# Feed-forward in a tuned encoder kernel: gate and up of seven chunks as a block product with seven half products

## The chip, the cores and the metric

The kernel runs on one core of a Trainium2 chip. The metric is the time of one execution on the device in microseconds. The kernel before takes 1268.14 us as the median of three runs (1267.69 to 1270.22).

TensorE is PE in the profile (its weight loads are PEld), VectorE is DVE, ScalarE is ACT, GpSimd is POOL and SyncE is SP.

## The reference

Two layers run over one sequence of 256 tokens with a width of 1024. Each layer is a half-step feed-forward, a mixer (a gated recurrence beside a forgetting attention), and a second half-step feed-forward. All is float32. The feed-forward is what matters here:

```
def rms_norm(x, g):
    y = x * rsqrt(mean(x * x, axis=-1) + EPS)
    return y * g

def swiglu_ffn(h, w_up, w_down):           # h 256 x 1024, D_FF = 2816
    gate, up = split(h @ w_up, 2, axis=-1) # w_up 1024 x 5632
    return (silu(gate) * up) @ w_down      # w_down 2816 x 1024

x = x + 0.5 * swiglu_ffn(rms_norm(x, g_ffn1[l]), w_up1[l], w_down1[l])
...                                        # the mixer
x = x + 0.5 * swiglu_ffn(rms_norm(x, g_ffn2[l]), w_up2[l], w_down2[l])
```

## The kernel before

**Products in float32.** TensorE multiplies a shortened format (`float32r`). So every operand is split into a high part and the rest, `hi` and `lo`, and a product is three matmuls: hi x hi, hi x lo, lo x hi (L398 to L400 in `visit`). The activations are split once, as `xT` (the tokens in the columns of the stationary operand, 128 at a time, so there are two token halves). The weights are the moving operand and are split as they come.

**Weight tiles.** `plan` and its callers put the weights of the whole program into one list, `hcs`, in the order of use. An entry is 512 KB: two blocks of 128 rows by 512 columns (a `raw` tile of 128 x 1024 elements). For each entry SP issues a load into one of four `raw` buffers (`emit_dma`, L299), ACT casts it to `whi` (`emit_hi`, L332), DVE subtracts that from `raw` to give `wlo` (`emit_lo`, L341) and with that frees the `raw` buffer for the next load. There are six `whi` and six `wlo` buffers. `can_hi` lets the cast of an entry be written out only after the entry six places before has been used by both token halves.

**Feed-forward.** `plan_ffn` and `ffn` go through six chunks of 512 of the 2816 inner columns (the last has 256). For each chunk, `block` makes the gate and then the up product: for each token half four weight tiles are summed into one PSUM bank. When a bank is full, `ev_g` applies silu with the scale rstd on ACT, and `ev_u` multiplies by the up product on DVE. `h_chain` turns the result (`turn`: a copy on ACT or DVE, a DMA transpose issued by SP, a copy back) and splits it. After the up product of chunk c (c from 1 to 4), `down` adds chunk c - 1 into four banks held through the whole feed-forward (`x` and `y`).

**What sets the order.** The program is written out by a planner, `Sched`, in Python. It keeps an expected time for PE, ACT, DVE and POOL, adds a fixed cost for each instruction it writes (`act_c`, `dve_c`), and works with generators: a `Chain` yields the time from which it is ready and the engine that it needs next. After each 512 columns of a weight tile `visit` calls `hook`, which first lets `split` cast and subtract the next weight tile, at most three ahead, then steps the chains that are ready, background ones (`bg`) only if their engine is not more than 2.5 us ahead, and then lets `split` go further ahead, up to the ring's size, if the engine has little to do. What comes out is one fixed list of instructions for each engine, and each engine runs its list strictly in that order.

**Buffers besides.** Twelve `slot` buffers of 8 KB per partition hold the larger tiles (`s0` to `s11` in the rows); four PSUM banks `z` serve gate, up and transposes. `rows_chain` loads the small constants through POOL into a slot, waits 70 us of planned time, and transposes them on PE.

## Time and profile before

| | |
|---|---|
| median of three runs | 1268.14 us |
| the profiled execution | 1271.76 us |
| its span | 1270.0 us |
| PE, PEld busy | 1255.3 us (99%), 1033.6 us (81%) |
| DVE, ACT busy | 824.9 us (65%), 826.8 us (65%) |
| DMA | 253.5 MB, 200 GB/s on average |

The span goes from the first to the last instruction of the program on the core; the execution's own time is 1.76 us longer. A busy share is an average over stages that differ much: feed-forward takes four stretches, each between two mixers or at the ends. Matmuls are pipelined, and the end of each is modelled, so rows of PE overlap and the start of one after the other is what a matmul costs. A wait is put down to what came last.

### The profile page before, as it was taken

What the parts mean: (1) busy time and instruction counts of PE and PEld (TensorE: products, weight loads), DVE (VectorE), ACT (ScalarE), POOL (GpSimd) and SP (SyncE); (2) the same over time, 40 slices, a digit from 0 to 9 for tenths busy, and PEclk for the clock granted to TensorE, in tenths of its full rate; (3) what the DMA queues carried; (4) which work ended last, traced back from release to release, by engine and by line L of the source; (5) the groups of instructions that cost most, each with busy time, mean ns of one, the idle gap of its engine ahead of it and who ended that gap; (6) DMA issues with size and microseconds to landing.
All of it is one profiled execution on the core that took longest, in us unless ns stands there. A gap on an engine that the chain in (4) does not pass through costs nothing.

```text
span 1270.0 us, 16219 instructions
## 1 busy us (share of the span) xinstructions
PE 1255.3 (99%) x5889; PEld 1033.6 (81%) x5889; DVE 824.9 (65%) x1158; ACT 826.8 (65%) x1086; POOL 68.6 (5%) x88
## 2 busy tenths in 40 slices
PE   9999999999999999999999999999999999999998
PEld 7887887788877888888878888878887778888887
DVE  6655556798777666555475555578987767655553
ACT  6657556886799456555566555569768984665553
POOL 4000000001400000000000000000032000000000
PEclk9999999999999999999999999999999999999999
DMA  7977769576567568667768677596676665687773
GB/s 252 247 212 217 223 173 257 142 222 208 166 174 188 178 190 212 205 213 206 193 195 238 199 207 207 157 276 163 203 218 156 184 189 174 200 223 215 215 189 102
DMA packets 212304, 253.50 MB, mean 200 GB/s; under 512 B 92488, under 2 KB 104960, under 8 KB 212224
## 3 DMA queue, kind: packets, MB, share of 16 engines
q1 hardware_dynamic: 210288, 249.21, 67.8%
q0 software_dynamic: 1920, 3.26, 1.2%
q8 instruction: 46, 0.75, 0.3%
q14 instruction: 34, 0.28, 0.1%
q10 hardware_dynamic: 16, 0.00, 0.0%
HBM read 229.88 MB, written 2.10 MB: 183 GB/s over the span
## 4 chain that ended last, share of the span: by engine, by line
PE 72%; DVE 5%; DMA 2%; issue 1%; ACT 1%; SPq 0%; DVEq 0%; ACTq 0%
PE x L398 11%; PE x L400 11%; PE x L399 11%; PE z L398 9%; PE z L400 9%; PE z L399 9%; PE y L398 3%; PE y L400 3%; PE y L399 3%; DVE wlo L341 2%; PE z L1010 1%; PE z L479 1%; PE y L1082 1%; DMA tmp<-in_b_gate_dram 1%; PE z L820 1%
## 5 line engine op out<-in xcount | busy, mean ns | idle before, releaser
L341 DVE TENSOR_TENSOR wlo<-raw,whi 128x1024 fp32r<-128x1024 f32 x423 | 510.2, 1221 | 220.6 <-ACT whi L332 213.3
L332 ACT CAST whi<-raw 128x1024 fp32r<-128x1024 f32 x423 | 439.5, 1048 | 208.4 <-PE z L400 122.0
L398 PE MATMUL x<-whi,s 128*128 128x512 f32 x800 | 323.3, 404 | 5.5 <-ACT s L500 2.4
L399 PE MATMUL x<-wlo,s 128*128 128x512 f32 x800 | 312.9, 391 | 0.8 <-DVE wlo L341 0.7
L400 PE MATMUL x<-whi,s 128*128 128x512 f32 x800 | 313.3, 392 | 0.1
L398 PE MATMUL z<-whi,s 128*128 128x512 f32 (+1 forms) x752 | 279.6, 372 | 1.0 <-ACT s L500 1.0
L399 PE MATMUL z<-wlo,s 128*128 128x512 f32 (+1 forms) x752 | 279.8, 372 | 0.1
L400 PE MATMUL z<-whi,s 128*128 128x512 f32 (+1 forms) x752 | 279.6, 372 | 0.0
L398 PEld LDWEIGHTS x<-whi,s 128*128 128x128 f32 x800 | 150.4, 188 | 40.9 <-ACT s L500 4.7
L400 PEld LDWEIGHTS x<-whi,s 128*128 128x128 f32 x800 | 150.4, 188 | 34.9 <-DVE s L502 2.5
L399 PEld LDWEIGHTS x<-wlo,s 128*128 128x128 f32 x800 | 150.6, 188 | 30.9 <-DVE wlo L341 2.0
L399 PEld LDWEIGHTS z<-wlo,s 128*128 128x128 f32 x752 | 141.8, 189 | 26.0 <-DVE wlo L341 1.8
L398 PEld LDWEIGHTS z<-whi,s 128*128 128x128 f32 x752 | 141.8, 189 | 25.6 <-ACT s L500 1.4
L400 PEld LDWEIGHTS z<-whi,s 128*128 128x128 f32 x752 | 141.8, 189 | 25.0 <-DVE s L502 0.8
L319 ACT COPY tmp<-nat 128x1024 uint16<-128x1024 uint16 (+1 forms) x88 | 96.3, 1114 | 75.9 <-DMA nat<-tmp 67.9
L398 PE MATMUL y<-whi,s 128*128 128x512 f32 x208 | 82.4, 396 | 0.0
L400 PE MATMUL y<-whi,s 128*128 128x512 f32 x208 | 81.1, 390 | 0.0
L399 PE MATMUL y<-wlo,s 128*128 128x512 f32 x208 | 81.1, 390 | 0.0
L640 DVE SCALAR_TENSOR_TENSOR nat<-z,rstd,nat 128x512 f32<-128x512 f32 (+1 forms) x48 | 33.9, 705 | 56.3 <-PE z L400 56.3
L502 DVE TENSOR_TENSOR s<-tmp,s 128x512 fp32r<-128x512 f32 (+1 forms) x71 | 46.6, 656 | 34.8 <-ACT s L500 34.4
L500 ACT CAST s<-tmp 128x512 fp32r<-128x512 f32 (+1 forms) x71 | 42.1, 594 | 28.1 <-DVE tmp L529 26.5
L635 ACT ACTIVATE nat<-z,rstd 128x512 f32<-128x512 f32 (+1 forms) x46 | 29.9, 651 | 45.1 <-PE z L400 45.0
(164 smaller groups left out, 903.1 us busy)
## 6 DMA issues: line engine op xcount, KB each, us to landing
raw<-in_w_up_dram SPq DMA_DIRECT2D x175, 512.0 KB, 4.7
...
```

Of the source, the lines that this page charges most:

```text
L319: nc.scalar.copy(out_, in_)
L332: nc.scalar.copy(hi, raws[i])
L341: nc.vector.tensor_tensor(out=lo, in0=raws.pop(i), in1=f32(hi), op=ALU.subtract)
L398: nc.tensor.matmul(acc, lhsT=lhs(0, k0 + kk)[:, ts], rhs=hi[:, kk, :], start=st, stop=False)
L399: nc.tensor.matmul(acc, lhsT=lhs(0, k0 + kk)[:, ts], rhs=lo[:, kk, :], start=False, stop=False)
L400: nc.tensor.matmul(acc, lhsT=lhs(1, k0 + kk)[:, ts], rhs=hi[:, kk, :], start=False, stop=sp)
L479: nc.tensor.transpose(dst_ps[:, j * P:(j + 1) * P], src[:, j * P:(j + 1) * P], ident)
L500: nc.scalar.copy(hi, t)
L502: nc.vector.tensor_tensor(out=lo, in0=t, in1=f32(hi), op=ALU.subtract)
L635: nc.scalar.activation(s[tok][0], acc, AF.Silu, scale=rs(tok))
L640: nc.vector.scalar_tensor_tensor(out=h, in0=acc, scalar=rs(tok), in1=h, op0=ALU.mult, op1=ALU.mult)
L820: nc.tensor.matmul(ps[:, g, :], lhsT=wax[0][:, g, n, :], rhs=xr[0][:, n, :], start=True, stop=True)
```

## The change

Gate and up of a chunk are seen as one product of 2 x 2 blocks: the activations are split by token half and by the upper and lower half of the 1024 inputs, the weights by that same half and by gate or up. The four result blocks (gate and up of each token half) are then made of seven products of blocks instead of eight, after the scheme of Strassen and Winograd. A product of blocks is here two weight tiles by one token half.

- `SEVEN` names the chunks: chunk 3 in the first feed-forward, chunks 2 and 4 in the other three.
- The weight blocks are `11` (gate, upper half), `12` (up, upper), `22` (up, lower), `21` (gate, lower). They are loaded straight into slots, in twos (`u` 0 and 1) of 512 KB, each two together with one of the `raw` loads ahead of them (`plan_seven`, `emit_dma`).
- `Seven.sums` makes on DVE t3 = 22 - 12, t1 = 12 - 11 (over `12`), t2 = t3 + 11 (over `11`, after `11` has been split) and t4 = 21 - t2 (over `21`, after that has been split). It starts as a background chain 6 us of planned time after the last load was written.
- The seven weights `11`, t1, t2, `21`, t3, `22`, t4 are split into `whi` and `wlo` like any tile: 14 entries instead of 8, each used by one product.
- `sums_chain` makes the four sums of activations once in each feed-forward, and splits them.
- In `seven(c)` the products come into `z` banks; ACT copies the first, DVE makes seven additions, and then silu, the multiplication and `h_chain` follow as before.
- `rows_chain` waits 25 us of planned time instead of 70.

```diff
@@ -48,6 +48,8 @@
+SEVEN = ((3,), (2, 4), (2, 4), (2, 4))
@@ -237,9 +239,77 @@
     def plan(w, r0, c0, nk, ncol):
-        hcs.append((w[r0:r0 + nk * P, c0:c0 + ncol].rearrange("(k p) n -> p k n", p=P), nk, ncol))
+        loads.append((w[r0:r0 + nk * P, c0:c0 + ncol].rearrange("(k p) n -> p k n", p=P), len(hcs)))
+        hcs.append((nk, ncol))
+        uses.append(NT)
+
+    ORDER = ("11", "t1", "t2", "21", "t3", "22", "t4")
...
+        def load(self, name, u, src):
...
+            nc.sync.dma_start(out=self.part(name, u), in_=src)
+            if name != "12":
+                raws[self.index(name, u)] = self.part(name, u), 0.0
+            if (name, u) == ("21", 1):
+                self.chain = S.add(self.sums(), S.now + 6.0, "d", True)
+
+        def sums(self):
+            def op(name, u, dst, a, b, f):
+                o = self.part(dst, u)
+                nc.vector.tensor_tensor(out=o, in0=self.part(a, u), in1=self.part(b, u), op=f)
+                raws[self.index(name, u)] = o, S.use("d", dve_c(1024))
+
+            for u in range(2):
+                op("t3", u, "t3", "22", "12", ALU.subtract)
+                yield S.now, "d"
+                op("t1", u, "12", "12", "11", ALU.subtract)
+                yield S.now, "d"
+            for name, dst, a, b, f in (("t2", "11", "t3", "11", ALU.add), ("t4", "21", "21", "11", ALU.subtract)):
+                for u in range(2):
+                    while nxt["lo"] <= self.index(dst, u):
+                        yield S.now + 0.5, "d"
+                    op(name, u, dst, a, b, f)
+                    yield S.now, "d"
...
+    def plan_seven(w, f0):
...
+        for name, r0, c0 in (("11", 0, f0), ("12", 0, FF + f0), ("22", 512, FF + f0), ("21", 512, f0)):
+            for u in range(2):
+                r = r0 + 256 * u
+                loads.insert(len(loads) - 3 + n // 2, (w[r:r + 256, c0:c0 + 512].rearrange("(k p) n -> p k n", p=P),
+                                                       (st, name, u)))
+                n += 1
+        for _ in range(14):
+            hcs.append((2, 512))
+            uses.append(1)
@@ -297,16 +370,18 @@
     def emit_dma(cuts=1):
...
+        while loads and isinstance(loads[0][1], tuple):
+            src, (st, name, u) = loads.pop(0)
+            st.load(name, u, src)
@@ -322,31 +397,33 @@
     def can_hi():
         i = nxt["hi"]
-        return i < NHC and i in raws and (i < RING or used[i - RING] == NT)
+        return i < NHC and i in raws and (i < RING or used[i - RING] == uses[i - RING])
...
-        emit_dma()
+        if uses[i] == NT:
+            emit_dma()
@@ -624,6 +706,115 @@
+        def sums_chain():
...
+            for q in range(2):
...
+                nc.vector.tensor_tensor(out=a[0][:, ks], in0=f32(xh[:, ks]), in1=f32(xl[:, ks]), op=ALU.add)
...
+            for i, u, v, f in ((0, A(1, 0), A(1, 1), ALU.add), (1, B(0), A(0, 0), ALU.subtract),
+                               (2, A(0, 0), A(1, 0), ALU.subtract), (3, A(0, 1), B(1), ALU.subtract)):
...
+                yield from split_seg(b[0][:, ii], sums[0][0][:, ii], sums[1][0][:, ii], 1024)
...
+        def seven(c):
...
+            def prod(name, lhs_, fin):
+                b, r = zbank()
+                for u in range(2):
+                    visit(st.index(name, u), b, lhs_, 2 * u, None, u == 0, u == 1, (lambda: fin(b, r)) if u else None)
...
+            def after_1(b, r):
+                nc.scalar.copy(s1, b)
...
+            def after_6(b, r):
+                plus(u2, b, s1)
+                r.free = True
+                plus(u4, b5[0], u2)
+
+            def after_2(b, r):
+                end = plus(s1, b, s1)
+                r.free = True
+                gate(0, s1, end)
+
+            def after_7(b, r):
+                plus(u2, b, u2)
+                r.free = True
+                plus(c22, b5[0], u2)
+                b5[1].free = True
+
+            def after_3(b, r):
+                end = plus(u4, b, u4)
+                r.free = True
+                up(0, u4, end)
+
+            def after_4(b, r):
+                end = plus(u2, b, u2)
+                r.free = True
+                up(1, c22, gate(1, u2, end))
+
+            prod("11", xh(0, 0), after_1)
+            prod("t1", xs(0), lambda b, r: b5.extend((b, r)))
+            prod("t2", xs(1), after_6)
+            prod("21", xh(0, 1), after_2)
+            prod("t3", xs(2), after_7)
+            prod("22", xs(3), after_3)
+            prod("t4", xh(1, 1), after_4)
...
@@ -1212,7 +1407,7 @@
-        yield S.now + 70.0, "p"
+        yield S.now + 25.0, "p"
```

**The order, place 1: DVE in the second feed-forward, from chunk 1's up block to the first weights of chunk 2.** Before, where `raw_810` to `raw_820` are tiles of the down product and `raw_825` is the first of chunk 2's gate:

```order
L341 TENSOR_TENSOR wlo_826_4286<-raw_810_4189,whi_822_4263 128x1024
L640 SCALAR_TENSOR_TENSOR nat_812_4216<-z_823_4265,rstd_107,nat_812_4216 128x512
L316 COPY tmp_830_4309<-nat_812_4216 128x1024
L341 TENSOR_TENSOR wlo_831_4318<-raw_816_4234,whi_829_4307 128x1024
L341 TENSOR_TENSOR wlo_835_4332<-raw_820_4252,whi_833_4322 128x1024
L640 SCALAR_TENSOR_TENSOR nat_821_4261<-z_828_4300,rstd_107,nat_821_4261 128x512
L341 TENSOR_TENSOR wlo_838_4345<-raw_825_4271,whi_834_4330 128x1024
L341 TENSOR_TENSOR wlo_841_4353<-raw_827_4288,whi_837_4343 128x1024
L341 TENSOR_TENSOR wlo_848_4395<-raw_832_4320,whi_845_4377 128x1024
```

After the change, in the same place. `raw_836`, `raw_842` and `raw_845` belong to the down product; `s4` holds `11` and then t2, `s8` holds `12` and then t1, `s0` holds `22`, `s3` holds t3, and `s1` will hold `21` and t4. Tiles are numbered in the text by the place of their `wlo` in DVE's list: that of `raw_836` is tile 169, `raw_842` and `raw_845` are 170 and 171, and the seven are 172 to 185 (the first two are the `wlo` from `s4` below). Chunk 1 has the tiles 160 to 167.

```order
L416 TENSOR_TENSOR wlo_852_4350<-raw_836_4253,whi_849_4337 128x1024
L279 TENSOR_TENSOR s3_832_4243<-s0_830_4241,s8_829_4240 128x1024
L279 TENSOR_TENSOR s8_829_4240<-s8_829_4240,s4_828_4239 128x1024
L279 TENSOR_TENSOR s3_832_4243<-s0_830_4241,s8_829_4240 128x1024
L831 SCALAR_TENSOR_TENSOR nat_838_4281<-z_848_4333,rstd_107,nat_838_4281 128x512
L279 TENSOR_TENSOR s8_829_4240<-s8_829_4240,s4_828_4239 128x1024
L416 TENSOR_TENSOR wlo_856_4383<-raw_842_4302,whi_855_4381 128x1024
L416 TENSOR_TENSOR wlo_861_4406<-raw_845_4315,whi_858_4393 128x1024
L831 SCALAR_TENSOR_TENSOR nat_847_4331<-z_854_4373,rstd_107,nat_847_4331 128x512
L416 TENSOR_TENSOR wlo_865_4423<-s4_828_4239,whi_860_4404 128x1024
L279 TENSOR_TENSOR s4_828_4239<-s3_832_4243,s4_828_4239 128x1024
L416 TENSOR_TENSOR wlo_868_4442<-s4_828_4239,whi_863_4417 128x1024
```

Five sums stand among the subtractions here, four of them ahead of tile 170, and every later `wlo` of DVE stands behind them.

**Place 2: DVE at the end of the same seven.** Here `s7` holds the four partial results, `z_889` is the product with t2, `z_885` with t1, `z_893` with `21`, `z_898` with t3, `z_902` with `22`; the last `wlo` of a seven is that of `s1` before `raw_851`, the first down tile (186).

```order
L757 TENSOR_TENSOR s7_879_4499<-z_889_4545,s7_879_4499 128x512
L757 TENSOR_TENSOR s7_879_4499<-z_885_4525,s7_879_4499 128x512
L416 TENSOR_TENSOR wlo_894_4570<-s3_832_4243,whi_888_4543 128x1024
L416 TENSOR_TENSOR wlo_896_4580<-s0_830_4241,whi_890_4552 128x1024
L757 TENSOR_TENSOR s7_879_4499<-z_893_4566,s7_879_4499 128x512
L416 TENSOR_TENSOR wlo_899_4592<-s0_830_4241,whi_892_4564 128x1024
L416 TENSOR_TENSOR wlo_900_4600<-s1_831_4242,whi_895_4575 128x1024
L757 TENSOR_TENSOR s7_879_4499<-z_898_4588,s7_879_4499 128x512
L757 TENSOR_TENSOR s7_879_4499<-z_885_4525,s7_879_4499 128x512
L416 TENSOR_TENSOR wlo_903_4613<-s1_831_4242,whi_901_4607 128x1024
L416 TENSOR_TENSOR wlo_905_4623<-raw_851_4345,whi_904_4618 128x1024
L757 TENSOR_TENSOR s7_879_4499<-z_902_4609,s7_879_4499 128x512
```

Additions that wait for a product of PE now stand between the `wlo` of the next products; before, each bank of four weight tiles was read by one instruction of ACT or DVE.

**Place 3: SP in the same stretch.** Before:

```order
L308 DMA raw_806_4180<-in_w_down2_dram 128x2x512
L308 DMA raw_810_4189<-in_w_down2_dram 128x2x512
L515 DMA_TRANSPOSE nat_790_4099<-tmp_811_4194 128x8x128
L308 DMA raw_816_4234<-in_w_down2_dram 128x2x512
L308 DMA raw_820_4252<-in_w_down2_dram 128x2x512
L308 DMA raw_825_4271<-in_w_up2_dram 128x2x512
L308 DMA raw_827_4288<-in_w_up2_dram 128x2x512
L515 DMA_TRANSPOSE nat_812_4216<-tmp_830_4309 128x8x128
L308 DMA raw_832_4320<-in_w_up2_dram 128x2x512
```

After; `x2` is two loads of 512 KB:

```order
L380 DMA raw_827_4237<-in_w_down2_dram 128x2x512
L270 DMA s4_828_4239<-in_w_up2_dram 128x2x512 x2
L380 DMA raw_836_4253<-in_w_down2_dram 128x2x512
L270 DMA s8_829_4240<-in_w_up2_dram 128x2x512 x2
L597 DMA_TRANSPOSE nat_807_4144<-tmp_837_4260 128x8x128
L380 DMA raw_842_4302<-in_w_down2_dram 128x2x512
L270 DMA s0_830_4241<-in_w_up2_dram 128x2x512 x2
L380 DMA raw_845_4315<-in_w_down2_dram 128x2x512
L270 DMA s1_831_4242<-in_w_up2_dram 128x2x512 x2
L380 DMA raw_851_4345<-in_w_down2_dram 128x2x512
```

Two loads of a seven follow each of four `raw` loads. In these rows the first transpose of h has six loads ahead of it, in those of before two.

## Rows read from the trace of the kernel before

**Rows 1.** The page: busy time by engine (part 1), TensorE's granted clock (part 2).

```profile
PE 1255.3 (99%) x5889; PEld 1033.6 (81%) x5889; DVE 824.9 (65%) x1158; ACT 826.8 (65%) x1086; POOL 68.6 (5%) x88
PEclk9999999999999999999999999999999999999999
```

**Rows 2.** The page, part 4: shares of the chain that ended last.

```profile
PE 72%; DVE 5%; DMA 2%; issue 1%; ACT 1%; SPq 0%; DVEq 0%; ACTq 0%
```

**Rows 3.** Busy time of each engine in two feed-forward windows; columns in the heading.

```profile
core 0: us, PE busy (x) PEld busy (x) DVE busy (x) ACT busy (x) POOL busy (x), PEclk, DMA share, GB/s
508.00:540.00 32.00, 32.00 (x142) 26.48 (x142) 17.74 (x17) 17.51 (x19) 0.00 (x0) 1.00 0.69 204
540.00:572.00 32.00, 32.00 (x143) 26.50 (x142) 17.74 (x17) 17.73 (x19) 0.00 (x0) 1.00 0.68 213
```

**Rows 4.** Timeline of PE in feed-forward: start us, us, engine, line, operation, tiles.

```profile
79.73 0.39 PE L398 MATMUL z<-whi,s 128*128 128x512 f32 x1
...
82.00 0.39 PE L399 MATMUL z<-wlo,s 128*128 128x512 f32 x1
```

**Rows 5.** Waits of the weight loads on VectorE: us in total, times, longest us.

```profile
PEld x L399 <- DVE wlo L341: 2.0, 3, 1.1
...
PEld z L399 <- DVE wlo L341: 1.8, 5, 0.5
```

**Rows 6.** Groups by line and shape: busy us, mean ns of one, idle before.

```profile
L341 DVE TENSOR_TENSOR wlo<-raw,whi 128x1024 fp32r<-128x1024 f32 x423 | 510.2, 1221 | 220.6 <-ACT whi L332 213.3
L332 ACT CAST whi<-raw 128x1024 fp32r<-128x1024 f32 x423 | 439.5, 1048 | 208.4 <-PE z L400 122.0 <-PE x L400 43.3 <-DMA raw<-in_w_in_dram 12.2
L640 DVE SCALAR_TENSOR_TENSOR nat<-z,rstd,nat 128x512 f32<-128x512 f32 x40 | 30.0, 750 | 45.9 <-PE z L400 45.9
L635 ACT ACTIVATE nat<-z,rstd 128x512 f32<-128x512 f32 x38 | 26.2, 689 | 43.4 <-PE z L400 43.4
L316 DVE COPY tmp<-nat 128x1024 uint16<-128x1024 uint16 x24 | 16.7, 698 | 5.7 <-DMA nat<-tmp 5.0
L1147 DVE TENSOR_TENSOR s<-x,s 128x512 f32<-128x512 f32 x8 | 5.5, 690 | 5.1 <-PE x L400 5.1
L885 DVE TENSOR_TENSOR s<-s,s 128x1024 f32<-128x1024 f32 x4 | 4.9, 1219 | 0.0
```

**Rows 7.** Timeline of VectorE in feed-forward: ops that follow without a gap.

```profile
66.69 1.23 DVE L341 TENSOR_TENSOR wlo<-raw,whi 128x1024 fp32r<-128x1024 f32 x1 [3.74 <-ACT whi L332]
67.83 0.68 DVE L502 TENSOR_TENSOR s<-tmp,s 128x512 fp32r<-128x512 f32 x1
68.43 1.22 DVE L341 TENSOR_TENSOR wlo<-raw,whi 128x1024 fp32r<-128x1024 f32 x1
...
88.08 2.35 DVE L341 TENSOR_TENSOR wlo<-raw,whi 128x1024 fp32r<-128x1024 f32 x2
```

**Rows 8.** Timelines in the recurrence: VectorE's chained ops, and PE's wait behind them.

```profile
263.58 0.69 DVE L850 TENSOR_TENSOR s<-s,s 128x512 f32<-128x512 f32 x1
264.31 0.69 DVE L851 TENSOR_TENSOR s<-s 128x512 f32<-128x512 f32 x1
...
269.69 0.50 PE L399 MATMUL x<-wlo,s 128*128 128x512 f32 x1 [0.72 <-DVE wlo L341]
```

**Rows 9.** Timeline of all engines: hand-over from a cast to the subtraction behind it.

```profile
72.45 1.05 ACT L332 CAST whi<-raw 128x1024 fp32r<-128x1024 f32 x1 [0.67 <-PE z L400]
...
73.53 2.59 DVE L341 TENSOR_TENSOR wlo<-raw,whi 128x1024 fp32r<-128x1024 f32 x2 [3.89 <-ACT whi L332]
```

**Rows 10.** DMA: a full queue's window, transposes' us to landing, ACT's wait, last constants' load.

```profile
8.00:12.00 4.00, 3.94 (x21) 2.72 (x19) 2.65 (x5) 1.79 (x3) 0.00 (x0) 1.00 1.05 401
...
nat<-tmp SPq DMA_TRANSPOSE x64, 4.6
...
ACT tmp L319 <- DMA nat<-tmp: 67.9, 27, 4.4
...
33.73 0.58 POOL L470 DMA_DIRECT2D bfb<-in_b_forget_dram  x1
```

More of the change, by code (lines that the diff above doesn't have):

```diff
@@ L299, in emit_dma @@
     def emit_dma(cuts=1):
-        i = nxt["dma"]
-        if i >= NHC:
+        if not loads:
             return
-        nxt["dma"] += 1
-        src, nk, ncol = hcs[i]
+        src, i = loads.pop(0)
+        nk, ncol = hcs[i]
         t = new(raw_p, [P, nk, ncol], "raw")
@@ L348, in split @@
             lead = 1
-        if can_hi() and nxt["hi"] - nxt["pos"] <= lead and (idle is None or S.busy("a") < idle):
+        if can_hi() and nxt["hi"] - nxt["pos"] <= lead and (
+                idle is None or S.busy("a") < idle) and raws[nxt["hi"]][1] <= max(S.now, S.t["a"]) + 0.05:
             emit_hi()
@@ L384, in get_hc @@
             if nxt["hi"] == nxt["lo"]:
+                for st in sevens:
+                    if st.i0 <= nxt["hi"] < st.i0 + 14:
+                        while nxt["hi"] not in raws:
+                            S.step(st.chain, True)
                 assert can_hi()
@@ L393, in visit @@
         hi, lo = get_hc(i)
-        _, nk, ncol = hcs[i]
-        ts = slice(tok * P, tok * P + P)
+        nk, ncol = hcs[i]
+        ts = slice(tok * P, tok * P + P) if tok is not None else slice(0, P)
         for kk in range(nk):
@@ L403, in visit @@
                 used[i] += 1
-                if used[i] == NT:
+                if used[i] == uses[i]:
                     ready.pop(i)
```

114 lines of the change are left out of this document (96 added, 18 removed).

## The prediction

> **What bounds the kernel now.** I read the page first: PE is busy 99% of the span against 65% each for DVE and ACT, and TensorE's granted clock shows no dip [rows 1]. A busy PE can still be a slow PE, so next came the chain of waits: 72% of it lies on PE [rows 2]. Then the feed-forward stretches, since only they change: in two windows of 32 us PE is busy throughout, DVE and ACT some 17.7 us each, with the DMA engines at 0.69 and 0.68 [rows 3]. The timeline of PE inside such a stretch shows what one matmul of 512 columns costs: from the start at 79.73 to that at 82.00 us there are ten steps, so 2.27 / 10 = 0.227 us each, although each row is drawn 0.39 us long [rows 4]. The list of PE's waits is short: over the whole span the weight loads waited 3.8 us for `wlo` [rows 5]. So feed-forward is bound by PE's issue rate, and DVE and ACT each have about 14 us of every 32 to spare. A removed matmul is worth 0.227 us until one of them is late.
>
> **What the change removes.** A pair of blocks (gate and up of one chunk) is 8 weight tiles x 2 token halves x 2 k x 3 = 96 matmuls; seven half products are 7 x 2 x 2 x 3 = 84. Twelve fewer in each of 1 + 2 + 2 + 2 = 7 chunks: 84 x 0.227 = 19.1 us. This is the most that the change can give.
>
> **What it adds, and where that lies.** Durations are from [rows 6]; a weight-tile sum is taken at the 1.22 us of the f32 128x1024 tensor_tensor of L885, an add from PSUM, or any 512-wide split, at the 0.69 us of L1147.
> DVE, per chunk: 8 sums and 6 further `wlo` (14 x 1.22 = 17.1 us), 7 adds (4.8 us): 21.9 us. Per feed-forward the sums of the activations and their split: 4 x 1.22 + 4 x 0.69 = 7.6 us. Together 7 x 21.9 + 4 x 7.6 = 184 us on 825, some 1009 us: about 80% of the span. The total fits; what counts is one chunk.
> ACT, per chunk: 6 casts and one copy, 6 x 1.05 + 0.6 = 6.9 us, and two casts per feed-forward. ACT spares 14 us in 32 [rows 3], so I cost it at nothing by itself; without that cover it would be 6.9 us a chunk.
> The activations' sums lie beside the first two chunks, which add nothing else to DVE's 17.7 us in 32: no cost (7.6 us in each feed-forward if the cover were gone). The early transposes of the constants' rows now stand behind 171 matmuls of PE, 39 us, and behind the start; the last DMA of these rows was issued at 33.73 us, 5 us before PE can be there [rows 10]: no cost, and a few us once if they land later.
>
> The chunk itself, taken in the second feed-forward, its chunk 2 (the stretch of the order shown above, with its tile numbers). Six `whi`/`wlo` buffers mean that the cast of a weight tile waits until PE has left the tile six before. Let PE leave tile 163, the last of chunk 1's gate. Then a silu (0.69), the cast of tile 169 (1.05) and its `wlo` (1.22) follow on ACT and DVE; the hand-overs are small (a cast from 72.45 to 73.50, its `wlo` at 73.53 [rows 9]); with three of them, the one from PE taken at 0.2 us, 3.2 us. Only then comes the first sum. From there to the `wlo` of tile 187, the second tile of the down product behind the seven, DVE has 8 sums, 18 `wlo`, 6 adds, 2 splits of h, 3 multiplications by rstd and one copy. PE meanwhile has 4 tiles used twice, 4 of down used twice, 14 half products and half of tile 186: 48 + 48 + 84 + 6 = 186 matmuls, 42.2 us.
> How long does DVE take? Its ops overlap at the seam: two `wlo` take 2.35 us, not 2.44; from 66.69 to 67.83 is 1.14 for a 1024, from 67.83 to 68.43 is 0.60 for a 512 [rows 7]. By these starts: 26 x 1.14 + 8 x 0.60 + 3 x 0.66 + 0.6 = 37.0 us. Slack: 42.2 - 3.2 - 37.1 = 1.9 us, if DVE never stands still.
> It does stand still. Walking the order row by row with PE freeing a tile each 1.36 us (6 x 0.227), I find 0.8 us before the first sum (ACT has another cast and a split ahead of that silu), 1.2 us before tile 176, 0.35 us in small pieces, and about 0.25 us where an add reads the one just before it: 2.6 us. So the chunk ends 0.7 us late.
> One more wait comes from SP. The weights of a seven are issued in twos with the down tiles ahead of them, so six DMAs of 512 KB go out together, and the transpose of h stands behind them in the same queue. At the 401 GB/s of a full queue 512 KB take 1.31 us; a transpose lands after a median 4.6 us in a queue that now holds about two such loads; four more ahead make it 4.6 + 4 x 1.31 = 9.8 us [rows 10]. ACT reaches the copy that waits for it (ahead of the casts of tiles 168 and 169, so of the first sum) about 2.7 us too early by my walk. As the 1.2 us before tile 176 and some of the rest are then absorbed, the late transpose adds 1.3 us: 2.0 us in all. This holds in chunk 2 of three feed-forwards; in the three chunks 4 and in chunk 3 of the first, the transpose that counts stands ahead of the loads, so 0.7 us.
> Sum of the stalls: 3 x 2.0 + 4 x 0.7 = 8.8 us. The walk has an error of its own, which the bounds hold: from below, the slack of 1.9 us covers all (no stall, 0); from above, DVE pays full durations, 26 x 1.22 + 8 x 0.69 + 3 x 0.75 + 0.7 = 40.2 us, which is 1.2 us late before any standing still, and with the transpose's 2.7 us on top 3.9 us a chunk, 27.3 us in all. I take 8.8, the walked value, since the rows nearest to it (two 1024 ops in 2.35 us) are of the same instruction.
> Change: -19.1 + 8.8 = -10.3 us. On the profiled execution's 1271.76 us (span 1270.0, 1.8 around it) that is 1261.5; it lies 3.6 us above the median of the three runs, 1268.14, which becomes **1257.8, say 1258 us**.
>
> **A rule against the sum.** When DVE works without a gap, the rows show two things: an op that does not need its neighbour starts 0.08 us before the neighbour's end [rows 7], and an op that reads the one before it (263.58, 264.31) starts 0.73 us after that for 0.69 us of duration [rows 8]. The Trainium skill, "VectorE: DVE Perf Modes", section "The DRAIN you can't avoid", says that the next op does not start until the pipe has emptied, and that only one that nothing holds starts earlier. If the waits of this stretch count as holding, every op costs at least what is drawn, the 40.2 us above; the trace agrees for the chained op alone, since each of the two `wlo` in 2.35 us has a wait for its cast too. It stands behind the third rival.
>
> **The rivals.**
> 1. DVE keeps up. The slack of 1.9 us holds and transposes land in time: no stall, or up to 0.4 us a chunk, 19.1 to 16.3 us gained, 1249 to 1252 us. For it: the feed-forward windows show DVE idle 14 us in 32 [rows 3]. Against it: that slack cannot be carried far ahead, six buffers are 8 us of half products.
> 2. The matmuls saved turn into waiting for `wlo`. At 2.0 us of stall in every chunk plus part of the 1.2 of full durations, 2.7 us each, the gain is used up: 1268 us; from 1263 to 1271 by 2 to 3.1 us a chunk. For it: in the one stretch of before where DVE was full for about 18 us (the small ops of the recurrence), PE waited 0.72 us for a `wlo` at 269.69 [rows 8], so a full DVE is felt at once.
> 3. Slower: DVE becomes the bound of the stretch. Full durations and the late transpose in each seven, 3.9 us against 2.7 saved: 7 x 1.2 = 8 us lost, 1276 us. It decides from 2.72 us of stall a chunk. For it: chained ops do pay in full, and ACT already waited 67.9 us in 27 places for transposes [rows 10]. Against it: the pairs at 2.35 us [rows 7].
>
> **Chances.** The forecast, 1252 to 1263 us, 0.55; rival 1, 0.17; rival 2, 0.18 (0.07 of it still faster by more than 0.2%, 0.11 within); rival 3, 0.10. 0.2%, 2.5 us, is about what a measurement of this kernel can tell from no change. So faster 0.79, same 0.11, slower 0.10. The range 1249 to 1268 leaves out rival 3 and the upper part of rival 2, and next to nothing below, since 84 matmuls are all there is to save.
>
> **What would show it.** PE's list loses 84 rows of 128x512 at an unchanged 0.227 us between starts. Each seven chunk shows a wait of PE for `wlo` in its last half products or in the down product behind it, 0.5 to 2 us, longest in chunk 2 of the later three feed-forwards. DVE's busy time rises to about 1009 us and in a window over a seven is nearly the window's length. ACT's copy of a transposed h waits longer where it follows the six loads. The forecast is wrong if these waits are absent (rival 1), if they pass 2.7 us (rival 3), or if PE waits somewhere else, for a sum whose weights have not landed.

## The result, and the profile after

The changed kernel takes 1286.32 us (median of 4 runs, 1283.26 to 1293.07), the kernel before 1269.18 us (four runs): a ratio of 1.0144, interval 1.0120 to 1.0167. The prediction was 1258 us, range 1249 to 1268: wrong in sign and by 28 us. The profiled execution took 1285.29 us, 13.5 us more than that of before.

The page first: busy time by engine (part 1) and the shares of the chain that ended last (part 4).

```profile
PE 1245.5 (97%) x5805; PEld 1013.8 (79%) x5805; DVE 987.9 (77%) x1336; ACT 870.0 (68%) x1144; POOL 70.4 (5%) x88
...
PE 60%; DVE 21%; DMA 10%; issue 5%; ACT 3%; SPq 0%; DVEq 0%; ACTq 0%
```

Against [rows 1, 2]: PE has the 84 matmuls fewer (5889 to 5805), DVE 163 us more. The 184 predicted were a sum of durations, and these grew by 183; busy time counts the seams where two ops overlap once. TensorE's granted clock shows as 9 in each slice, as before, but a slice of 32 us hides short falls, on which more below. The chain has gone from PE to DVE (5% to 21%) and to DMA (2% to 10%). So PE waits, and not for DVE alone.

The windows of [rows 3], and three narrower ones around the first seven of the second feed-forward:

```profile
core 0: us, PE busy (x) PEld busy (x) DVE busy (x) ACT busy (x) POOL busy (x), PEclk, DMA share, GB/s
508.00:540.00 32.00, 28.01 (x116) 20.86 (x115) 31.76 (x34) 22.40 (x25) 0.00 (x0) 1.00 0.22 51
540.00:572.00 32.00, 31.36 (x139) 25.63 (x138) 21.56 (x21) 17.73 (x20) 0.00 (x0) 1.00 0.99 336
483.00:497.00 14.00, 14.00 (x63) 11.58 (x63) 5.02 (x6) 3.59 (x5) 0.00 (x0) 1.00 1.06 304
497.00:505.00 8.00, 8.00 (x37) 6.63 (x36) 4.74 (x5) 6.20 (x7) 0.00 (x0) 1.00 1.04 401
520.00:541.00 21.00, 17.63 (x70) 12.24 (x69) 20.83 (x22) 13.00 (x15) 0.00 (x0) 1.00 0.06 15
```

Read them in order of time. From 483 to 505 us the DMA engines are full and DVE works 10 us of 22: it could have made the sums then, but their weights are on the way. From 520 to 541 the DMA engines are nearly idle, DVE is full, and PE has gaps. An even 204 GB/s [rows 3] has become a heap and a gap.

The waits (us in total, times, longest), where [rows 5] had 2.0 and 1.8 us:

```profile
PEld z L481 <- DVE wlo L416: 27.1, 34, 3.1
PE z L481 <- DVE wlo L416: 14.4, 20, 2.7
PEld x L481 <- DVE wlo L416: 14.1, 13, 2.1
DVE s L279 <- DMA s<-in_w_up_dram: 12.0, 4, 4.3
PE x L481 <- DVE wlo L416: 8.9, 11, 1.7
```

The fourth line is new: L279 is the sum of weights, and four of the seven first sums stood at a load: 4.27 us in the first feed-forward, 2.90, 0.69 and 4.15 in the three chunks 4. The groups by form, for [rows 6]:

```profile
L416 DVE TENSOR_TENSOR wlo<-raw,whi 128x1024 fp32r<-128x1024 f32 x367 | 441.1, 1220 | 99.1 <-ACT whi L407 96.3
L416 DVE TENSOR_TENSOR wlo<-s,whi 128x1024 fp32r<-128x1024 f32 x98 | 116.6, 1217 | 0.4 <-ACT whi L407 0.4
L279 DVE TENSOR_TENSOR s<-s,s 128x1024 f32<-128x1024 f32 x56 | 67.9, 1222 | 13.1 <-DMA s<-in_w_up_dram 12.0
L757 DVE TENSOR_TENSOR s<-z,s 128x512 f32<-128x512 f32 x49 | 33.6, 685 | 0.5
```

Every duration is the one the prediction used (1.22, 1.22, 0.69). The pace of PE, for [rows 4]:

```profile
490.75 0.39 PE L481 MATMUL z<-wlo,s 128*128 128x512 f32 x1
...
492.34 0.39 PE L482 MATMUL z<-whi,s 128*128 128x512 f32 x1
```

Seven steps in 1.59 us: 0.227 us each, as before. The prices were right; what stands between the instructions was not.

**One number for each seven.** Count the `wlo` of DVE in order to number the weight tiles; let a be a seven's first. The *lag* is the time from PE's end on tile a-9 (the prediction's tile 163) to the first sum. The *stall* is what PE needs from that end to its first matmul with the `wlo` of tile a+15, less its 186 matmuls (42.2 us) and the one ahead of it. Both come from the timelines of PE and DVE.

| seven | predicted lag / stall | measured lag / stall |
|---|---|---|
| FFN 1, chunk 3 | 4.0 / 0.7 | 8.6 / 3.5 |
| FFN 2 to 4, chunk 2 | 6.7 / 2.0 | 11.2, 10.5, 10.1 / 6.9, 6.4, 5.7 |
| FFN 2 to 4, chunk 4 | 4.0 / 0.7 | 7.7, 7.1, 8.5 / 2.6, 2.7, 3.4 |

The stalls sum to 31.2 us, predicted were 8.8; 19.1 are saved. From the first sum to the `wlo` of tile a+15 DVE takes 37.2 to 38.2 us in all seven, close to what was predicted from there (37.0 and 1.8 of standing still), and lag + 37.5 - 42.2 gives each stall to 0.6 us. The first sum comes 3 to 5 us too late.

Why in chunk 2: SP's queue, ACT and DVE in the second feed-forward (start us, us, engine, line, operation; in brackets the idle time before and its releaser).

```profile
484.68 0.65 SPq L380 DMA_DIRECT2D raw<-in_w_down_dram  x1
485.43 2.01 SPq L270 DMA_DIRECT2D s<-in_w_up_dram  x2
487.53 5.01 SPq L597 DMA_TRANSPOSE nat<-tmp  x1
492.63 0.71 SPq L380 DMA_DIRECT2D raw<-in_w_down_dram  x1
...
489.53 1.04 ACT L407 CAST whi<-raw 128x1024 fp32r<-128x1024 f32 x1
497.42 1.35 ACT L394 COPY tmp<-nat 128x1024 uint16<-128x1024 uint16 x1 [6.85 <-DMA nat<-tmp]
...
500.22 0.69 DVE L584 TENSOR_TENSOR s<-tmp,s 128x512 fp32r<-128x512 f32 x1 [8.13 <-ACT s L582]
500.83 2.35 DVE L416 TENSOR_TENSOR wlo<-raw,whi 128x1024 fp32r<-128x1024 f32 x2
503.10 3.61 DVE L279 TENSOR_TENSOR s<-s,s 128x1024 f32<-128x1024 f32 x3
```

The transpose of h, issued behind the loads, keeps SP for 5.0 us instead of about 1.2 (622.57 in experiment 5), and ACT's copy behind it starts 9.9 us after its issue: the prediction said 9.8. But ACT stood there 6.85 us, not 2.7, and DVE behind it 8.13. Why in chunk 4: DVE in the second feed-forward, and the median us to landing by kind of DMA.

```profile
565.04 1.22 DVE L416 TENSOR_TENSOR wlo<-raw,whi 128x1024 fp32r<-128x1024 f32 x1 [2.02 <-ACT whi L407]
569.17 3.62 DVE L279 TENSOR_TENSOR s<-s,s 128x1024 f32<-128x1024 f32 x3 [2.90 <-DMA s<-in_w_up_dram]
```

```profile
s<-in_w_up_dram SPq DMA_DIRECT2D x56, 512.0 KB, 8.1
...
nat<-tmp SPq DMA_TRANSPOSE x64, 5.4
```

A seven's weights land 8.1 us after their issue, transposes 5.4 instead of 4.6 [rows 10]. In the third feed-forward only 0.69 us of the lag is a load: there the first sum stands in DVE's list behind the multiplication that ends the up product of the chunk ahead, and that waits for PE (experiment 5 shows such a place).

Two smaller losses outside the sevens: in the first feed-forward the sums of x stand on DVE ahead of a `wlo` that PE needs, and at the end of the second PE waits for the h of the last chunk.

```profile
17.36 2.35 DVE L721 TENSOR_TENSOR s<-s,s 128x1024 f32<-128x1024 f32 x2
...
20.90 0.50 PE L481 MATMUL x<-wlo,s 128*128 128x512 f32 x1 [1.71 <-DVE wlo L416]
...
635.04 0.50 PE L480 MATMUL x<-whi,s 128*128 128x512 f32 x1 [2.00 <-ACT s L582]
```

What PE's steps of over 0.3 us from one 512-wide matmul to the next start take beyond 0.227 us sums to 61.2 us after and 28.7 before: +32.5. Less the 19.1 saved this is 13.4 us; the span grew by 13.5. So the loss is waiting of PE, most of it in the sevens (31.2 us).

### The profile page after: what moved, and what is told of

The parts are those of the page before. It is cut to its first block, busy times and chain, and to the rows that moved or that the text cites. A ratio compares the mean times of both kernels' runs of the same rounds, so it can differ in the third digit from the quotient of the medians.

```text
span 1283.6 us, 16293 instructions
## 1 busy us (share of the span) xinstructions
PE 1245.5 (97%) x5805; PEld 1013.8 (79%) x5805; DVE 987.9 (77%) x1336; ACT 870.0 (68%) x1144; POOL 70.4 (5%) x88
## 4 chain that ended last, share of the span: by engine, by line
PE 60%; DVE 21%; DMA 10%; issue 5%; ACT 3%; SPq 0%; DVEq 0%; ACTq 0%
DVE wlo L416 12%; PE x L480 10%; PE x L481 10%; PE x L482 10%; PE z L481 6%; PE z L480 6%; PE z L482 6%; DMA s<-in_w_up_dram 3%; DMA nat<-tmp 3%; DVE s L279 3%; PE y L480 2%; PE y L482 2%; PE y L481 2%; DVE s L757 2%; DMA raw<-in_w_up_dram 2%
## 5 line engine op out<-in xcount | busy, mean ns | idle before, releaser
L416 DVE TENSOR_TENSOR wlo<-raw,whi 128x1024 fp32r<-128x1024 f32 x367 | 441.1, 1220 | 99.1 <-ACT whi L407 96.3
L407 ACT CAST whi<-raw 128x1024 fp32r<-128x1024 f32 x367 | 378.1, 1047 | 171.7 <-PE x L482 44.3
L481 PE MATMUL z<-wlo,s 128*128 128x512 f32 (+1 forms) x724 | 272.5, 376 | 14.5 <-DVE wlo L416 14.4
L480 PE MATMUL z<-whi,s 128*128 128x512 f32 (+1 forms) x724 | 269.4, 372 | 0.0
L482 PE MATMUL z<-whi,s 128*128 128x512 f32 (+1 forms) x724 | 269.2, 372 | 0.0
L481 PEld LDWEIGHTS z<-wlo,s 128*128 128x128 f32 x724 | 136.8, 189 | 49.6 <-DVE wlo L416 27.1
L480 PEld LDWEIGHTS z<-whi,s 128*128 128x128 f32 x724 | 136.9, 189 | 23.8
L482 PEld LDWEIGHTS z<-whi,s 128*128 128x128 f32 x724 | 136.8, 189 | 22.4
L416 DVE TENSOR_TENSOR wlo<-s,whi 128x1024 fp32r<-128x1024 f32 x98 | 116.6, 1217 | 0.4 <-ACT whi L407 0.4
L407 ACT CAST whi<-s 128x1024 fp32r<-128x1024 f32 x98 | 98.6, 1048 | 5.7 <-PE y L482 3.3
L279 DVE TENSOR_TENSOR s<-s,s 128x1024 f32<-128x1024 f32 x56 | 67.9, 1222 | 13.1 <-DMA s<-in_w_up_dram 12.0
```

The lines of the kernel that those rows point to most:

```text
L279: nc.vector.tensor_tensor(out=o, in0=self.part(a, u), in1=self.part(b, u), op=f)
L407: nc.scalar.copy(hi, raws[i][0])
L416: nc.vector.tensor_tensor(out=lo, in0=raws.pop(i)[0], in1=f32(hi), op=ALU.subtract)
L480: nc.tensor.matmul(acc, lhsT=lhs(0, k0 + kk)[:, ts], rhs=hi[:, kk, :], start=st, stop=False)
L481: nc.tensor.matmul(acc, lhsT=lhs(0, k0 + kk)[:, ts], rhs=lo[:, kk, :], start=False, stop=False)
L482: nc.tensor.matmul(acc, lhsT=lhs(1, k0 + kk)[:, ts], rhs=hi[:, kk, :], start=False, stop=sp)
```

## The experiments

Each kernel is the changed one with the edit shown, or its main line; a feed-forward without a seven makes no sums of x. Ratios are to the kernel before, run beside it. "Stall" is the sum over the run's sevens. The time of a feed-forward or mix is that between the last updates of x of two neighbours in the profiled execution.

**1. Weights in sooner or by another queue.** Spread over more raw loads:

```
-loads.insert(len(loads) - 3 + n // 2, ...
+loads.insert(len(loads) - 7 + n, ...
```

> The change with the eight loads of a seven put one by one behind the last eight raw loads ahead of it, instead of in twos behind the last four. DVE's work is the same. Theory A (the loads come late and in a heap, so the first sum starts 7 to 11 us after PE leaves the tile nine before the seven): the first sum starts 4 to 6 us after it, PE's stretch to the second down tile falls from 44 to 48 us to 42 to 44, and the time is 1260 to 1270 us. Theory B (DVE's own 37 to 38 us of work for a seven set the wait, wherever the loads stand): the stretch keeps its 44 to 48 us, the time 1280 to 1287.

1291.81 us, 1.0187 (1.0161 to 1.0212). Lags of 8.8 to 12.5 us, stall 39.6: no gain. No sum stands at a load any more, yet the lag grows: what comes ahead of the first sum waits in its place, as DVE here, in the second feed-forward ahead of chunk 4, for a transpose.

```profile
563.44 0.75 DVE L391 COPY tmp<-nat 128x1024 uint16<-128x1024 uint16 x1 [3.77 <-DMA nat<-tmp]
```

Issued by GpSimd:

```
-nc.sync.dma_start(out=self.part(name, u), in_=src)
+nc.gpsimd.dma_start(out=self.part(name, u), in_=src)
```

> The change with the loads of the sevens issued by POOL instead of SP; they then wait for their slots alone, not for DVE's freeing of raw buffers, and no transpose of h stands behind them. Theory A: the first sum starts 4 us after PE leaves the tile nine before, the copy of h no longer waits 5 to 6 us, PE waits under 1 us a chunk, time 1254 to 1264 us. Theory B: the wait of PE for wlo in each seven stays, time 1280 to 1287 us.

1281.4 us, 1.0100 (1.0077 to 1.0123). No first sum stands at a load. In chunks 3 and 4 the lag falls to 3.9 to 6.3 us and the stall to 1.8 to 1.9; in chunk 2 the lag stays at 8.5 to 10.2, since ACT still stands at its copy (4.08 us in the second feed-forward). Stall 22.7. Two chunks 4 have the lag that was forecast (4.2 and 3.9 us), and still stall 1.9 us, not 0.7: DVE stands longer inside the seven, for ACT's casts, and takes 40.1 and 40.4 us. DVE in the first of them, and SP in the first feed-forward:

```profile
582.50 2.59 DVE L416 TENSOR_TENSOR wlo<-s,whi 128x1024 fp32r<-128x1024 f32 x2 [1.42 <-ACT whi L407]
586.02 1.23 DVE L416 TENSOR_TENSOR wlo<-s,whi 128x1024 fp32r<-128x1024 f32 x1 [0.94 <-ACT whi L407]
...
65.99 9.96 SPq L597 DMA_TRANSPOSE nat<-tmp  x1
```

The last row is a transpose issued with three of SP's loads and seven of GpSimd's in flight. So a queue of their own does not keep loads out of a transpose's way.

The first sum's operands first:

```
-(("11", 0, f0), ("12", 0, FF + f0), ("22", 512, FF + f0), ("21", 512, f0))
+(("22", 512, FF + f0), ("12", 0, FF + f0), ("11", 0, f0), ("21", 512, f0))
```

> The change as it is, but each seven loads its quarters in the order 22, 12, 11, 21 instead of 11, 12, 22, 21, so that the operands of the first sum (22 less 12) are the first to land. Theory A: in chunks 3 and 4 the first sum waits for 22 no longer; their lag falls by about 2 us and their stall by as much, 4 x 1.5 = 6 us: 1278 to 1283 us; chunk 2's lag, which hangs on the transposed h, stays over 9 us. Theory A3 (the heap is late as a whole; the next sum waits for 11 in place of the first for 22): the first sum starts earlier but a gap of 2 us or more stands inside VectorE's stretch, 1284 to 1290 us.

1283.21 us, 1.0115 (1.0100 to 1.0131). Chunks 3 and 4: lags of 4.2 to 6.3 us, stalls of 1.9 to 2.8; chunk 2 as before (11.0 to 11.6). Half of what theory A wanted: DVE's stretch grew to 38.8 to 40.1 us. The gap of theory A3 is there too: in three of the four a later sum stood 1.8 to 2.7 us at a load.

**2. Which sevens cost.** Without chunk 2, then chunk 2 alone, then none:

```
-SEVEN = ((3,), (2, 4), (2, 4), (2, 4))
+SEVEN = ((3,), (4,), (4,), (4,))
+SEVEN = ((), (2,), (2,), (2,))
+SEVEN = ((), (), (), ())
```

> Sevens in chunk 3 of the first feed-forward and in chunk 4 of the other three only; chunk 2 as before. Theory A: the dear chunks are the chunks 2, where the transpose of h stands behind the loads; the four left stall 1.8 to 2.7 us each against 2.7 saved, so 1265 to 1270 us. Theory B: every seven costs alike, 17.1 / 7 = 2.4 us net, so 1269 + 4 x 2.4 = 1279 us.

1268.49 us, 1.0001 (0.9988 to 1.0014): stall 9.2, against 10.9 saved; single waits take the rest (1.9 us at the sums of x, 1.6 at the last chunk's h of the second feed-forward).

> Sevens in chunk 2 of the last three feed-forwards only. Theory A: 4.9 to 6.0 us of stall each against 2.7 saved, so 1269 + 8 = 1277 us (1274 to 1279). Theory B: 1269 + 3 x 2.4 = 1276 us; the two agree here, and the run checks that the costs of the chunks add up.

1280.15 us, 1.0087 (1.0068 to 1.0107): lags of 10.3 to 10.9, stall 18.2 against 8.2 saved; 10.0 more, and 11 measured. Chunk 2 carries the loss.

> The change with no seven at all (every chunk a plain gate and up): what is left of it is the vectors' transposes planned 25 us after the rows' loads instead of 70 us. In the runs so far the first feed-forward and the first mix together took 455.7 us where no seven stood in them, 459.5 us before. Theory D (this move alone is worth those 3.8 us, and the sevens cost more than the total shows): 1264 to 1266 us. Theory E (those 3.8 us come from something else): 1267 to 1270 us.

1269.33 us, 1.0001 (0.9992 to 1.0011). The earlier transposes of the constants are worth nothing. The first 460 us differ by up to 4 us between profiled executions, and part of that goes with TensorE's granted clock: in the execution of before it was 0.50 (1.2 GHz, else 2.4) from 225.93 to 229.34 us, just after PE had waited 1.48 us for ACT; here it shows no such fall.

**3. ACT's place for the copy of h.** A longer time planned for the transpose, everywhere:

```
-yield end + 6.0, "a"
+yield end + 11.0, "a"
```

> The change as it is, but the planner counts 11.0 us instead of 6.0 us for the transpose of h, so that ScalarE's copy of the transposed h is put later in ScalarE's order, behind the casts of the seven; the loads stay on SP. Theory A (two delays ahead of the first sum: the loads land late, and in chunk 2 ScalarE stands at the copy of a transpose that SP issued behind six loads): chunk 2 loses the second of the two, so its lag falls from 10.1 to 11.2 us to the 7 to 8.6 us of chunk 4 and its stall from 4.9 to 6.0 us to about 2: 3 x 3.5 = 10 us off, 1273 to 1279 us; the lag of chunks 3 and 4 stays at 7 to 8.6 us. Theory A2 (SP's queue of loads alone makes the lag, and the copy only waits beside it): the lag of chunk 2 stays over 9 us, 1283 to 1289 us. Theory B (VectorE's 37 to 38 us of work sets the wait): no change, 1284 to 1288 us.

1286.27 us, 1.0135 (1.0115 to 1.0154). Chunk 2's stalls fall from 5.7 to 6.9 to 2.7 to 3.2 us, all seven from 31.2 to 20.8, as theory A said; the time stays. The mixes use the same planner, and the second took 263.0 us instead of 259.1, the first 1.3 us more. The four feed-forwards give back only 3.1 of the 10.4 us: in the second PE waits 2.14 us at the last chunk's h, and then the granted clock is 0.50 for 6.8 us.

> The same longer allowance of 11.0 us for the transpose, and the seven's loads issued by GpSimd instead of SP. Theory A: both delays are gone; the lag of every seven chunk is 4 to 6 us, chunk 2's stall falls from the 3.4 to 5.3 us of the run with GpSimd loads alone to about 1.5 us: 1281 less 3 x 3 = 1272 us, 1267 to 1275 us. Theory A2 (only the loads' landing counts): as with GpSimd loads alone, 1279 to 1284 us. Theory B: 1279 to 1284 us.

With GpSimd's loads as well: 1289.16 us, 1.0171 (1.0145 to 1.0196); stall 20.2, first feed-forward 202.7 us (198.6 in the change), mixes 263.3 and 263.6. Inconclusive for the same reason.

Next, only in the chunk ahead of a seven (10.0 where `c + 1 in SEVEN[no]`):

> The change as it is (loads on SP), with 10.0 us instead of 6.0 us planned for the transpose of h only in the chunk ahead of a seven; the mixes stay as they are. With the allowance longer everywhere chunk 2's stretch on TensorE fell from 47.1 to 48.2 us to 44.1 to 44.6 us, but the mixes took 5 us longer and the time stayed. Theory A (the copy of the transposed h in ScalarE's order makes chunk 2's lag): 3 x 3.4 = 10 us off, 1274 to 1279 us. Theory C (the stall moves to another wait of the same feed-forward): 1283 to 1288 us.

1286.74 us, 1.0138 (1.0123 to 1.0154), lags in chunk 2 of 10.6 to 12.8. A miss of mine: the copy that blocks is of the h of chunk 0. So 11.0 where `c + 2 in SEVEN[no]`:

> The change as it is, with 11.0 us planned for the transpose of h only in the feed-forward chunk two ahead of a seven (the last run lengthened it in the chunk next to it, but the copy at which ScalarE stands for 6 to 8 us ahead of chunk 2's first sum is that of chunk 0). Mixes and loads as in the change. Theory A (this copy makes chunk 2's lag): TensorE's stretch at chunk 2 falls from 47.1 to 48.2 us to 44 to 45 us, 3 x 3.3 = 10 us off, 1274 to 1279 us. Theory C (the stall turns into another wait of the same feed-forward): the stretch falls and the time stays, 1283 to 1288 us.

1279.83 us, 1.0077 (1.0053 to 1.0101): 6.5 us off the change, stall 24.5 (31.2). ACT and DVE ahead of the same seven:

```profile
495.35 1.05 ACT L407 CAST whi<-raw 128x1024 fp32r<-128x1024 f32 x1 [1.20 <-DMA raw<-in_w_down_dram]
496.30 0.62 ACT L582 CAST s<-tmp 128x512 fp32r<-128x512 f32 x1
499.05 1.35 ACT L394 COPY tmp<-nat 128x1024 uint16<-128x1024 uint16 x1 [2.13 <-DMA nat<-tmp]
...
501.09 0.69 DVE L584 TENSOR_TENSOR s<-tmp,s 128x512 fp32r<-128x512 f32 x1 [1.44 <-ACT s L582]
501.70 2.48 DVE L279 TENSOR_TENSOR s<-s,s 128x1024 f32<-128x1024 f32 x2
```

The copy waits 2.13 us instead of 6.85, with the casts ahead of it; the lag is 8.4 (11.2). Chunk 2's three stalls sum to 10.9 us, 19.0 in the change. The first sum here still stands behind the split of that h, not at a load; only in the third feed-forward is there a load, 0.75 us.

**4. Is it DVE's length?** The eight sums on GpSimd, sevens in chunks 3, 4, 4, 4:

```
-nc.vector.tensor_tensor(out=o, in0=self.part(a, u), in1=self.part(b, u), op=f)
+nc.gpsimd.tensor_tensor(out=o, in0=self.part(a, u), in1=self.part(b, u), op=f)
```

> Sevens in chunks 3, 4, 4, 4, with the eight sums of weights of each computed by GpSimd instead of VectorE, loads on SP. VectorE loses 8 x 1.14 = 9.1 us of each seven's 37 us. Theory B (once the first sum has started, VectorE's length is what is left of the stall): TensorE's stretch falls from 43.2 to 44.5 us to 42.2 to 42.5 us, 1263 to 1266 us against the 1268.5 us of the run with VectorE's sums. Theory A (the loads' landing and the casts set the rest): the stretch stays at 43 to 45 us, 1267 to 1271 us. If one sum on GpSimd takes over 3.3 us, GpSimd is the bound instead: over 1271 us.

1301.75 us, 1.0248 (1.0231 to 1.0265), the opposite of theory B. GpSimd and DVE in the second feed-forward:

```profile
568.62 11.91 POOL L279 TENSOR_TENSOR s<-s,s 128x1024 f32<-128x1024 f32 x4 [98.54 <-DMA s<-in_w_up_dram]
...
568.75 2.83 DVE L392 COPY tmp<-nat 128x1024 uint16<-128x1024 uint16 x1
571.51 6.77 DVE L417 TENSOR_TENSOR wlo<-raw,whi 128x1024 fp32r<-128x1024 f32 x2
```

A sum takes GpSimd 3.0 us in this row, 3.2 in the mean of 32, and beside it a `wlo` takes DVE 3.4 instead of 1.2 and a copy 2.83 instead of 0.76. DVE's work is not shortened, it is locked out. (GpSimd is near the 3.3 us at which it was to be the bound; the two were not told apart.) The Trainium skill, "SBUF — State Buffer", section "SBUF: two separate sides", says that the two share a pair of ports which one holds for its whole instruction; the trace agrees.

**5. The first sum early, and the seven's place.** First, loads by GpSimd at their old place in the list: sevens in 3, 4, 4, 4 with the sums of x at 24 us (`S.now + 24.0` for `S.now + 4.0`), then in chunk 4 of the last three feed-forwards alone.

> Sevens in chunks 3, 4, 4, 4 alone (no chunk 2), their loads issued by GpSimd, and the sums of x planned 24 us after the start of the feed-forward instead of 4 us. Theory A: the run without chunk 2 took 1268.5 us with 6.0 us of stalls in the four sevens; GpSimd loads leave about 1 us each (43.2 to 43.3 us of TensorE's stretch against 42.2), so 2 us off, and the 1.9 us that TensorE waited in the first feed-forward for the sums of x go too: 1261 to 1266 us, below the kernel before (1268 us). Theory C (what the sevens save is given back elsewhere, through DMA traffic in bursts, whatever their own stalls): 1266 to 1272 us.

1273.17 us, 1.0033 (1.0016 to 1.0051). The last three feed-forwards took 546.1 us (547.9 without these edits, 548.5 before), the first 202.2 (197.9): there a transpose kept SP 7.19 us with seven of GpSimd's loads in flight, and ACT waited up to 4.45 us for raw weights.

> One seven (chunk 4) in the second, third and fourth feed-forward, none in the first, loads by GpSimd. Put together from stages of other runs: first feed-forward and first mix 455.7 us (the run with chunk 2 alone), the rest 804.7 us (the run with chunks 3, 4, 4, 4 and GpSimd loads), ahead of what follows the last stage 1260.4 us: 1261 to 1264 us, below before. Theory C (what the sevens save comes back elsewhere): 1265 to 1270 us.

1268.26 us, 0.9995 (0.9981 to 1.0010); each lag 6.3 us, each stall 1.8. No load is waited for: 6.3 us is the place in DVE's list, behind the multiplication of the chunk ahead:

```profile
567.05 0.75 DVE L831 SCALAR_TENSOR_TENSOR nat<-z,rstd,nat 128x512 f32<-128x512 f32 x1 [2.55 <-PE z L482]
567.72 3.61 DVE L279 TENSOR_TENSOR s<-s,s 128x1024 f32<-128x1024 f32 x3
```

Then all eight loads four tiles earlier, on the whole change:

```
-loads.insert(len(loads) - 3 + n // 2, ...
+loads.insert(len(loads) - 7 + n // 2, ...
```

> The change as it is, with all eight loads of each seven's weights placed four tiles earlier in the queue of loads, two at a time as before. Theory A (the loads land too late for the first sum): the first sum of chunks 3 and 4 comes within 4 us of TensorE's leaving of the ninth tile ahead, their stretch falls from 43.9 to 44.9 us to 42.5 to 43.3 us, and chunk 2 gains too, since its transpose of h meets no heap: 1270 to 1278 us. Theory F (the floor is the ring of six tiles and VectorE's 37 us, which casts in ScalarE's order interrupt): the first sum comes earlier, VectorE's stretch grows by the same, and TensorE's stays over 43 us in every seven: 1280 to 1287 us.

1321.1 us, 1.0418 (1.0392 to 1.0445). The first sum comes early in chunk 2 (lags of -3.9 to 0.3 us), but on SP the loads now hold back everything behind them: three transposes of the second feed-forward kept SP 5.20 to 6.31 us, ACT's casts waited 58.7 us for raw tiles of `w_up` (30.2 in the change), and the stall is 63.0. TensorE's granted clock was 0.982 in the mean (0.998).

The same with GpSimd's queue and one seven (chunk 4), two and four tiles earlier:

> One seven (chunk 4) in the second to fourth feed-forward, loads by GpSimd and two tiles earlier. Theory A: the three stretches fall from 43.21 us to 42.2 to 42.5 us, 3 x 0.8 = 2.4 us off the 1268.3 us of the same kernel with later loads: 1264 to 1267 us. Theory F: the stretches stay at 43.2 us and the time at 1267 to 1270 us.

> As the run before, with the loads four tiles earlier. Theory A: as before, 1263 to 1267 us. Theory F: stretches of 43.2 us, 1267 to 1270 us.

1275.45 us, 1.0054 (1.0033 to 1.0075), and 1272.39 us, 1.0032 (1.0014 to 1.0049). The stalls did what theory A said, but for the first: 2.8, 1.0, 1.0 with lags of -1.7 us, and 0.8 three times with lags of -7.7 to -7.8. Theory F's floor falls. (Earlier loads move two things at once: the landing, and the sums' place in DVE's list, as the planner starts them 6 us after the last load.) Yet the time did not follow. PE in the second feed-forward of the last kernel, and SP there:

```profile
597.78 0.39 PE L480 MATMUL x<-whi,s 128*128 128x512 f32 x1
598.80 0.50 PE L481 MATMUL x<-wlo,s 128*128 128x512 f32 x1 [0.63 <-DVE wlo L416]
...
624.98 0.39 PE L482 MATMUL x<-whi,s 128*128 128x512 f32 x1
628.31 0.80 PE L480 MATMUL x<-whi,s 128*128 128x512 f32 x1 [2.94 <-ACT s L582]
...
616.93 5.59 SPq L380 DMA_DIRECT2D raw<-in_w_up_dram  x3
622.57 1.21 SPq L597 DMA_TRANSPOSE nat<-tmp  x1
...
628.29:631.70 3.41, 3.39 (x8) 2.72 (x9) 0.84 (x2) 0.00 (x0) 0.00 (x0) 0.50 0.12 16
```

The first two rows are all that is left of the stall (0.8 us); the next two are a wait at the first product of the last chunk's h, where PE already stood 2.00 us in the second feed-forward of the change. Its transpose is issued 2.4 to 3.8 us after that chunk's last gate and up matmul; before, 1.4 us ahead of it. A seven ends with both halves' h at once, and their copies and transposes go ahead of the last chunk's. PE stood 3.1, 2.5 and 1.9 us there. The last row, a window with the columns of those above, is what followed: TensorE's granted clock at 0.50 for 3.4 us, with 8 matmuls, so 0.43 us each, some 1.6 us lost. The same came after the second wait (816.02 to 819.43 us), none after the third. Over the 12 executions of this kernel the time goes with the clock: 1268.6 to 1270.2 us in the four with 0.999 or more, 1274.6 to 1279.2 in the four longest, with 0.995 to 0.997. One chunk earlier, with the sums of x at 24 us:

```
+SEVEN = ((), (3,), (3,), (3,))
```

> One seven in the second to fourth feed-forward at chunk 3 instead of chunk 4, loads by GpSimd and four tiles earlier, sums of x planned 24 us after the start of the feed-forward. With the seven at chunk 4 and loads as early, TensorE's stretch was 42.19 us, the whole stall gone, but TensorE stood 3.1, 2.5 and 1.9 us at the first product of the last chunk's h: SP issued that h's transpose 2.4 to 3.8 us after the chunk's last gate and up matmul, 1.4 us before it in the kernel before. Theory G (a seven ends with both tokens' h at once, and their copies and transposes push the last chunk's behind them; one chunk earlier they fall where TensorE has other work): these waits go, the stretches stay near 42.2 us, and the 3 x 2.7 us saved show: 1259 to 1263 us. Theory C (the saving is given back at whatever comes next): 1266 to 1271 us.

1267.23 us, 0.9992 (0.9982 to 1.0001): the lowest ratio, not told apart from before or from e10. The waits at the last chunk are gone (the transpose is again 1.4 us ahead), the stalls stay at 0.8. Theory G holds for the place and fails for the size. The last three feed-forwards take 544.6 us, 3.9 less than before: 8.2 saved, 2.4 in stalls, and 1.3 of a wait behind the sums of x in the third:

```profile
675.31 0.39 PE L480 MATMUL z<-whi,s 128*128 128x512 f32 x1
677.04 0.50 PE L481 MATMUL z<-wlo,s 128*128 128x512 f32 x1 [1.34 <-DVE wlo L416]
```

Last, the sums of x at 50 us:

> As the run before (a seven at chunk 3 of the second to fourth feed-forward, loads by GpSimd four tiles earlier), with the sums of x planned 50 us instead of 24 us after the start of the feed-forward. In the run before they stood on VectorE ahead of two casts of plain tiles in the third feed-forward, and TensorE waited 1.7 us there. Theory G (what is left of the saving is lost at single waits that can be moved away): the third feed-forward falls from 183.4 to about 182 us, and the time by 1.5 us to 1264.5 to 1267 us. Theory C: the wait comes up elsewhere, 1267 to 1269 us.

1271.24 us, 1.0016 (1.0002 to 1.0029). The wait came up again and larger, as theory C said:

```profile
699.51 0.39 PE L480 MATMUL z<-whi,s 128*128 128x512 f32 x1
702.32 0.50 PE L481 MATMUL z<-wlo,s 128*128 128x512 f32 x1 [2.42 <-DVE wlo L416]
```

## Why the prediction was wrong

- **What is saved** (84 matmuls, 19.1 us): right. 0.227 us between starts held, and where the stall was taken away PE crossed the stretch in 42.19 us plus 0.8 (predicted 42.2).
- **DVE's length** (37.0 us of starts and 1.8 of standing still from the first sum on): the starts are right; 37.2 to 38.2 in the change. The standing was mis-sized, hidden by the late start: at the lag that was forecast (e2) DVE takes 40.1 and 40.4 us, and the stall is 1.9 us where 0.7 were said.
- **The failed step is the lag**: a silu, the cast of tile 169 and its `wlo`, 3.2 us, and 0.8 more, so 4.0, and "Only then comes the first sum". The walk took the weights as landed by then. In chunks 3 and 4 they were not: the lag was 7.1 to 8.6 us, and 4.3, 2.9, 0.7 and 4.2 of it a wait for a load. The SP queue's six loads were counted against the transpose alone, never against the sums that need those same loads. e2 takes that wait away, and the four stalls fall from 12.2 to 7.5 us (2.8 predicted). Of the rest, part is the standing just named, part the place behind a multiplication. With the sums earlier still (e15, e16) the stall falls to 1.0 and 0.8 us at lags of -1.7 and -7.7.
- **The late transpose in chunk 2**: right as a mechanism and in its landing (9.8 us predicted, 9.9 measured), mis-sized at ACT. "About 2.7 us too early by my walk" measured 6.85. Of the 1.3 us counted for it in each, e13 shows more: with the copies two chunks ahead of a seven put later, chunk 2's three stalls fall by 8 us and the time by 6.5.
- **The activations' sums at no cost**: wrong by 1.9 us in the first feed-forward (2.10 between two starts for 0.227). The average of 14 us of idle DVE in 32 says nothing on where it is idle: e17 and e18 moved the sums twice and PE waited at each place.
- **No term for the last chunk**: the sum had nothing for what a seven in chunk 4 hands on late; in the change this is 2.2 us in the second feed-forward.
- **Rival 3** had the sign and the place, by other numbers: full durations and 3.9 us a chunk, 1276 us. The stalls were 2.6 to 6.9, from late data, not from longer ops; the seam of 0.08 us stays (two `wlo` in 2.35 us), so the cited rule did not decide. The last words of the prediction, "for a sum whose weights have not landed", named what happened, without a price or a chance.

What stays open: why the saving that e17 shows in its three feed-forwards (3.9 us) is 1.2 us in the medians. The first 460 us vary by as much between executions, in part with the granted clock, whose falls were not set apart by a run of their own.
